# A hybrid decoder layer: the recurrent heads' values and gates from seven block products ahead of the heads, and their elementwise work spread over three engines

## The chip, the core and the metric

The kernel runs on one core of a Trainium2 chip. TensorE (PE) multiplies matrices and turns tiles (a transpose is a matmul with the identity), with its weight loads shown apart (PEld). VectorE (DVE), ScalarE (ACT) and GpSimd (POOL) do elementwise work, SyncE (SP) issues DMAs. PE writes into PSUM, 8 banks of 128 x 512 floats; DVE and ACT read it. The rest lives in SBUF, 128 partitions wide. The metric is the device time of one execution in microseconds. It is compared as a median of several runs; the profile is of one execution.

## What is computed

One decoder layer for 1024 tokens of width 1024, in float32. The part in front of the feed-forward block has two mixers side by side, fed by one projection of the normalised input:

```python
h = rmsnorm(x, mix_pre_norm)
proj = h @ w_in
q_a, k_a, v_a, q_h, f_h, i_h, g_h = split(proj)      # 3 x 512 attention, 4 x 512 recurrence
attn = rmsnorm(dilated_mixture_attention(q_a, k_a, v_a), attn_out_norm)
rec = hgrn2_recurrence(q_h, f_h, i_h, g_h, lb, hgrn_out_norm)
x = x + rmsnorm(concat([attn, rec]) @ w_out, mix_post_norm)
x = x + rmsnorm(square(relu(rmsnorm(x, mlp_pre_norm) @ w_ff1)) @ w_ff2, mlp_post_norm)
```

The recurrence has 4 heads of 128 columns; `f` is the forget gate per key column, `i` the values, `g` the output gate:

```python
f = lb + (1 - lb) * sigmoid(f_h)
S[t] = diag(f[t]) @ S[t-1] + outer(1 - f[t], i[t])
o[t] = S[t].T @ silu(q_h[t])
y = rmsnorm_per_head(o) * silu(g_h)
```

## The kernel before

The order of all instructions is written out by hand; there is no scheduler that moves them. Each engine runs its own list in order and waits on semaphores.

**Three-pass products.** A float32 operand is split into a rounded part `hi` (ACT copies it into the float32r type) and a rest `lo` (a subtraction, on DVE where nothing else is said): `split_into`, L82 to L84. A product is then hi x hi + hi x lo + lo x hi, three matmuls (`three_pass`, L87 to L89). Weights come as a `stream` of 512 KB pieces: `w_load` issues a DMA, `w_split` splits a piece, `w_get(i)` makes sure that piece i, and the next one, are split.

**Opening (0 to 39 us).** The 8 row tiles of x (`xr`, 128 x 1024) are turned by PE as they are (`x_turn`, L257); ACT and DVE take the turned tiles out as `hTh` and `hTl`, scaled by the norm's gain per column. The norm's factor per row, `rstd0`, is only ready later and is multiplied into what is projected: per token block for i and gate, and as a whole row tile `rrow` for q, f and the attention's projections. In the same stage head 0's i and gate columns are made, `pig`, 128 tokens x 256 columns at a time over 8 k: 192 matmuls of 128 x 256.

**Recurrent heads (39 to 307 us).** `hgrn_ig(h)` makes a head's i and gate, `hgrn_qf(h)` its q (with silu, `qt`) and f (`kt`, `tot`, and `prod` = qt x kt). A 1024-token projection of 128 columns, `proj_t`, is 2 halves x 8 k x 3 = 48 matmuls of 128 x 512. `hgrn_core(h)` is the recurrence. In heads 0 to 2 it joins the tokens in three steps by four (c = 1, 4, 16): at each step `quarter_sets` prepares the right-hand sides `qs` (ACT copies, L404 and L408; DVE products with the running gates `tot`, L409 and L411), PE makes 8 score blocks `pl` (L441), DVE copies them under masks into `at` (`copy_predicated`, L473), and DVE scales `qt` (L454, L457), makes the joined gates (L461 to L463) and scales `kt` (L466 to L468). Head 3 goes by two in seven levels (L502 to L513). After the steps come the transposed keys `pk`, state updates `pu` and `st` (L538), the output `po` (L549, L551), its squares `ysq`, and the gated, normalised result (L563), sent to DRAM.

The head's own matmuls wait for DVE between steps. So `fill(ns)` weaves other matmuls between them: it takes pieces from generators in `queue`, each piece one k step with its cost in ns, until the given time is used up. In head h the generators are `hgrn_ig(h+1)` and `hgrn_qf(h+1)`; in head 3 the first attention pair's projections, `attn_proj(0)`. The steps' `sets` of the next step are made before the masked copies of this one.

**After 307 us** follow the attention (to 555), the output projection (to 631), the feed-forward's two products (to 1207.6) and the last norm. The change touches of these only how attention's q, k and v leave PSUM.

Of the kernel before, what the change touches and what calls it, by code (L numbers as in the profile page):

```python
# [17 lines left out]
P = 128  # L18
# [9 lines left out]
LEVELS = (1, 2, 4, 8, 16, 32, 64)  # L28


def f32(ap):
    return ap.bitcast(F32)
# [3 lines left out]
def hymba_layer(ctx, tc, x, w_in, w_out, w_ff1, w_ff2, g_pre, lb_logits, g_mix, g_post,  # L36
# [10 lines left out]
    ps = ctx.enter_context(tc.tile_pool(name="psum", bufs=1, space=PSUM))  # L47
    dp = ctx.enter_context(tc.tile_pool(name="spill", bufs=1, space=DRAM))
# [5 lines left out]
    def bank(tag, name):  # L54
        return ps.tile([P, 512], F32, tag=tag, name=name,
                       bufs={"mm": 2, "s": 2, "t": 2, "pv": 2}[tag])
# [66 lines left out]
    def w_get(i, ahead=1):  # L123
        while done[1] < min(i + 1 + ahead, len(stream)):
            w_split()
        return parts[i]

    def pair_dest(name):
        box = {}

        def dest(j):
            def make():
                if j == 0:
                    box["h"] = slab("V8", f"{name}h", F32R, (P, 2, T))
                    box["l"] = slab("V8", f"{name}l", F32R, (P, 2, T))
                return box["h"][:, j], box["l"][:, j]
            return make
        return dest, box

    def ig_view(box, k):  # L140
        return tuple(box[q].rearrange("p j (k c) -> p j k c", k=NK)[:, :, k] for q in ("h", "l"))

    wig = []
    for h in range(HH):
        dest, box = pair_dest(f"wig{h}")
        wig.append(box)
        for j in range(2):
            stream.append((w_in[4 * h + j], dest(j)))
        for j in range(2):
            stream.append((w_in[4 * h + 2 + j], None))  # L150
    for i in range(4 * HH, 4 * HH + 3 * (AH // 2)):
        stream.append((w_in[i], None))
# [51 lines left out]
    hT = blocks_of("hT")  # L204
# [3 lines left out]
    xrows = [slab("S", f"xr{t}") for t in range(NT)]  # L208

# [3 lines left out]
    nc.sync.dma_start(out=ident, in_=ident_in)  # L213
    x_load(0)
    nc.sync.dma_start(out=gpre, in_=g_pre)
    w_load()
    w_load()
    for t in range(1, NT):
        x_load(t)
    V.memset(ones, 1.0)  # L220
    V.memset(nhalf, -0.5)
    rrow = slab("R", "rrow")
    mraw = slab("T", "mraw", F32, (P, len(LEVELS), 64))
    nc.sync.dma_start(out=lbl, in_=lb_logits)
    nc.sync.dma_start(out=mraw, in_=level_masks)

    mix_dram = dp.tile([T, D], F32, name="mixd")
    x2_dram = [dp.tile([P, D], F32, name=f"x2d{t}") for t in range(NT)]

    def ig_evac(hd, pm, blocks):  # L230
        for u, t in enumerate(blocks):
            S.activation(hd["inat"][:, t], pm[:, u, 0], AF.Copy, scale=rstd0[:, t:t + 1])
            V.tensor_scalar(hd["gate"][:, t], pm[:, u, 1], rstd0[:, t:t + 1], None, op0=ALU.mult)

    def silu_gate(h, gate):
        sg = slab("P", f"sg{h}", F32, (P, NT, P))
        S.activation(sg, gate, AF.Sigmoid)
        V.tensor_tensor(out=gate, in0=gate, in1=sg, op=ALU.mult)

    def new_head(h):  # L240
        return {"inat": slab("T", f"inat{h}", F32, (P, NT, P)), "gate": slab("T", f"gate{h}", F32, (P, NT, P))}

    heads = [None] * HH
    heads[0] = new_head(0)

    PAIRED = ((0, 1), (2, 4), (3, 5), (6, 7))
    pms0 = [bank(tag, f"pig0_{q}").rearrange("p (t j c) -> p t j c", t=2, j=2)
            for q, tag in enumerate(("mm", "mm", "pv", "pv"))]
    place = {t: pms0[q][:, u] for q, pair in enumerate(PAIRED) for u, t in enumerate(pair)}
    turned = [0]  # L250

    def x_turn(t0, n, k):
        hi, lo = part_tok(hT, k, t0, n)
        pt = bank("t" if turned[0] % 2 else "s", f"xt{t0}_{k}")[:, :n * P]
        turned[0] += 1
        for j in range(n):
            TE.transpose(pt[:, j * P:(j + 1) * P], xrows[t0 + j][:, k * P:(k + 1) * P], ident)  # L257
        S.activation(hi, pt, AF.Copy, scale=gpre[:, k:k + 1])
        V.scalar_tensor_tensor(lo, pt, gpre[:, k:k + 1], f32(hi), op0=ALU.mult, op1=ALU.subtract)

    def x_mm(t0, n, k):
        for t in range(t0, t0 + n):
            three_pass(place[t], part_tok(hT, k, t), ig_view(wig[0], k), k == 0, k == NK - 1)

    def squares(t0, n):
        for t in range(t0, t0 + n):
            dump = slab("P", f"sq{t}")
            S.activation(dump, xrows[t], AF.Square, accum_out=ssq0[:, t:t + 1])

    def row_scale(hf):  # L270
        sl = slice(hf * 512, hf * 512 + 512)
        pt = bank("t", f"rb{hf}")
        for j in range(4):
            t = hf * 4 + j
            TE.transpose(pt[:, j * P:(j + 1) * P], rstd0[:, t:t + 1].to_broadcast([P, P]), ident)
        S.activation(rrow[:, sl], pt, AF.Copy)

    def keep_warm(n):

        for _ in range(n):  # L280
# [1615 lines left out]
```

## Time and profile before

| what | us |
| --- | --- |
| median of 3 runs (lowest, highest) | 1261.32 (1260.96, 1261.83) |
| span of the profiled execution | 1258.5 |
| opening ends (head 0's i and gate done) | 39.3 |
| head 0's core begins | 62.5 |
| heads 1, 2, 3 begin | 125.2, 188.7, 252.1 |
| attention begins | 307.1 |
| output projection, ff1, ff2 begin | 555.0, 631.0, 941.0 |

The span runs from the first to the last instruction; about 2.8 us of the median lie around it. The stages are read off PE's list: where the matmuls of one name give way to those of the next. In the profile's rows `L87 PE MATMUL f<-bh,ah 128*128 128x512` means line 87, engine, operation, the tile written and those read, the stationary tile and the moving one; `x392` counts them, and the time of "idle before" belongs to the engine just before such an instruction, with what ended it. `PEclk` and the last columns of a stage row are the granted clock of PE, the busy share of the DMA engines and the GB/s they moved.

### The profile page before, as it was taken

The numbers are of one execution on the slowest core, as the hardware profiler recorded it, in microseconds if no ns is written. First come the engines' busy times: TensorE is split into PE (matmuls) and PEld (weight loads), VectorE is DVE, ScalarE is ACT, GpSimd is POOL, SyncE is SP. The second block draws the span as 40 slices with busy tenths as digits, with TensorE's granted clock in tenths as the row PEclk, the third lists the DMA queues.
The fourth block names the chain that finished last, engine by engine and source line by source line (L and its number), as shares of the span: only waits on it lengthen the run. The fifth ranks groups of instructions, "written<-read, shape, count | busy, mean of one in ns | idle before, by whom it ended". The sixth has DMA issues, their size and how long they took to land. (4 is left out here: it accounts for less than half of the span.)

```text
span 1258.5 us, 17252 instructions
## 1 busy us (share of the span) xinstructions
PE 1235.4 (98%) x6512; PEld 1056.1 (84%) x6512; DVE 884.6 (70%) x1535; ACT 531.9 (42%) x970; POOL 300.6 (24%) x303
## 2 busy tenths in 40 slices
PE   8999999999999999999999999999999999999997
PEld 8898989888888887878878788888878888888886
DVE  5686868675666667668759756666685777698966
ACT  7523232222555556666565322222237434444412
POOL 0000000012222223146250487656621000000012
PEclk9999999999999999999999999999999999999999
DMA  5201111122322224245242545434468454434423
GB/s 210 68 18 51 34 52 34 35 84 64 89 71 81 69 83 132 81 133 184 101 150 81 207 164 184 155 135 172 149 249 324 167 198 134 162 92 132 162 89 118
DMA packets 58578, 153.98 MB, mean 122 GB/s; under 512 B 4992, under 2 KB 12928, under 8 KB 58240
## 3 DMA queue, kind: packets, MB, share of 16 engines
q1 hardware_dynamic: 58496, 152.89, 36.0%
q8 instruction: 51, 0.84, 0.3%
q14 instruction: 31, 0.25, 0.1%
HBM read 106.73 MB, written 39.85 MB: 116 GB/s over the span
## 5 line engine op out<-in xcount | busy, mean ns | idle before, releaser
L87 PE MATMUL f<-bh,ah 128*128 128x512 f32 x392 | 152.5, 389 | 0.0
L88 PE MATMUL f<-bl,ah 128*128 128x512 f32 x392 | 152.5, 389 | 0.0
L89 PE MATMUL f<-bh,al 128*128 128x512 f32 x392 | 152.5, 389 | 0.0
L84 DVE TENSOR_TENSOR al<-ar,ah 128x1024 fp32r<-128x1024 f32 x49 | 60.7, 1238 | 48.1 <-ACT ah L83 19.4
L89 PEld LDWEIGHTS f<-bh,al 128*128 128x128 f32 x392 | 73.6, 188 | 15.4
L87 PEld LDWEIGHTS f<-bh,ah 128*128 128x128 f32 x392 | 73.6, 188 | 15.3
L88 PEld LDWEIGHTS f<-bl,ah 128*128 128x128 f32 x392 | 73.6, 188 | 15.1
L83 ACT ACTIVATE ah<-ar 128x1024 fp32r<-128x1024 f32 x49 | 52.1, 1063 | 50.2 <-PE f L89 25.3
L1814 POOL TENSOR_SCALAR fp<-fss 128x1 f32<-128x1 f32 x8 | 3.7, 462 | 269.4 <-ACT fd L1810 269.4
L734 DVE TENSOR_TENSOR ptl<-pt,pth 128x512 fp32r<-128x512 f32 (+2 forms) x96 | 50.4, 553 | 23.4 <-ACT pth L733 23.3
L733 ACT ACTIVATE pth<-pt 128x512 fp32r<-128x512 f32 (+2 forms) x96 | 43.3, 487 | 40.0 <-PE pt L730 38.5
L706 DVE CUSTOM_DVE_ANT_0 p<-ps,bt 128x512 f32<-128x512 f32 (+2 forms) x84 | 44.4, 554 | 18.3 <-PE ps L704 18.1
L1313 POOL TENSOR_TENSOR e<-x,e 128x512 f32<-128x512 f32 x14 | 20.6, 1475 | 136.0 <-DVE x L1264 136.0
L79 POOL TENSOR_SCALAR ms<-hss 128x8 f32<-128x8 f32 x4 | 0.8, 198 | 209.2 <-DVE hss L554 209.2
L717 ACT ACTIVATE p<-p,nm 128x128 f32<-128x128 f32 (+3 forms) x64 | 49.4, 772 | 2.5 <-DVE nm L710 2.1
L83 ACT ACTIVATE bh<-br 128x1024 fp32r<-128x1024 f32 x28 | 29.8, 1064 | 43.1 <-PE f L89 37.7
L763 POOL TENSOR_TENSOR anat<-anat,rd 128x128 f32<-128x128 f32 x32 | 14.7, 461 | 131.8 <-DVE anat L762 130.9
L730 PE MATMUL pt<-ident,p 128*128 128x128 f32 x288 | 42.7, 275 | 2.7 <-DVE ptl L734 1.6
L747 PE MATMUL pov<-pth,v 128*128 128x256 f32 (+1 forms) x160 | 40.3, 287 | 1.3 <-ACT pth L733 1.3
L1667 DVE TENSOR_TENSOR acc<-f,acc 128x512 f32<-128x512 f32 x52 | 33.8, 686 | 8.2 <-PE f L89 8.2
L730 PEld LDWEIGHTS pt<-ident,p 128*128 128x128 f32 x288 | 33.3, 141 | 7.2 <-DVE ptl L734 3.5
L83 ACT ACTIVATE bh<-tt 128x1024 fp32r<-128x1024 f32 x21 | 22.3, 1061 | 38.2 <-PE f L89 22.9
(1622 smaller groups left out, 3902.3 us busy)
## 6 DMA issues: line engine op xcount, KB each, us to landing
ar<-actd SPq DMA_DIRECT2D x49, 512.0 KB, 3.7
raw<-in_w_in_dram SPq DMA_DIRECT2D x28, 512.0 KB, 3.6
w1r<-in_w_ff_dram SPq DMA_DIRECT2D x14, 1024.0 KB, 6.2
br<-in_w_ff_dram SPq DMA_DIRECT2D x14, 1024.0 KB, 7.9
actd<-e SPq DMA_DIRECT2D x17, 768.0 KB, 4.1
actd<-e SPq DMA_DIRECT2D x11, 1024.0 KB, 4.0
xr<-in_x_dram SPq DMA_DIRECT2D x8, 512.0 KB, 8.6
raw<-in_w_out_dram SPq DMA_DIRECT2D x8, 512.0 KB, 3.6
```

What stands on the lines that cost most here:

```text
L83: S.activation(hi, src, AF.Copy)
L84: eng.tensor_tensor(out=lo, in0=src, in1=f32(hi), op=ALU.subtract)
L87: TE.matmul(dst, lhs[0], rhs[0], start=start, stop=False)
L88: TE.matmul(dst, lhs[0], rhs[1], start=False, stop=False)
L89: TE.matmul(dst, lhs[1], rhs[0], start=False, stop=stop)
L706: V.tensor_tensor_reduce(out=pe[:, k0:k0 + n], in0=pS[:, :n], in1=bts[hd][:, o:o + n], scale=1.0, scalar=-3.0e38, op0=ALU.add, op1=ALU.max ...
L717: S.activation(pe[:, :nk], pe[:, :nk], AF.Exp, bias=nm[:, b:b + 1], accum_out=dn[:, b:b + 1])
L730: TE.transpose(pt[:, j * P:(j + 1) * P], pe[:, jj * P:(jj + 1) * P], ident)
L733: S.activation(hi, src, AF.Copy)
L734: V.tensor_tensor(out=lo, in0=src, in1=f32(hi), op=ALU.subtract)
L747: TE.matmul(po[:, c0:256], vst, pt[j // 4][q][:, j % 4, c0:], start=j == 0 and q == 0, stop=j == nj - 1 and q == 1)
L1667: V.tensor_tensor(out=acc_at(p, i), in0=pm, in1=acc_at(p, i), op=ALU.add)
```

## The change

- **Rows first.** Each row tile is squared (ACT, tile 1 on DVE), its factor is made on POOL, and the row is scaled by DVE before PE turns it. `rrow` and all multiplications with it go.
- **Seven block products.** i and gate of all four heads are one product of 1024 tokens x 1024 by 1024 x 1024 columns. It is cut into 2 x 2 blocks of 512 and made by seven block products instead of eight (Strassen's scheme in Winograd's form): sums and differences of blocks of the rows (`s1` to `s4`) and the weights (`T1` to `T4`), split like every operand, then 7 x 4 token tiles x 4 k x 3 passes. The weight differences T3, T2 and T4 and the row sums are POOL's (`w_diff`, `a_rebuild`, L495, L505), the splits' rests DVE's. The results, i and silu(gate), go to DRAM (`i_dram`, `g_dram`); `head_load` reads a head's columns back as `inat` and `gate`.
- **Less to weave.** `hgrn_ig` is gone. In head h only f of head h+1 and q of head h+2 are left to weave in, and in head 2 two units of the attention's projection. A table, `FILLING`, gives each place its own time.
- **Heads' elementwise work.** The products `prod` and qt x tot, and the three scalings of `kt` per step, go to POOL; f's affine steps to ACT. The gating is made by ACT copies with a scale and a POOL product, and put off into the next head's first step. `ysq` is summed by ACT. The score blocks lie in pairs of banks, so that one masked copy takes 128 x 256. Head 3 goes by four, too.

```diff
+FILLING = (
+    dict(f0=1300.0, f1=700.0, st=(5400.0, 5400.0, 3400.0), f6=1300.0, pk=1400.0, pu=1400.0, po=700.0, end=700.0),
...
+    dict(f0=700.0, f1=0.0, st=(6100.0, 6100.0, 5400.0), f6=1300.0, pk=2000.0, pu=1400.0, po=700.0, end=700.0),
+    def w_diff(dst, in0, in1, eng, which=(0, 1)):
+        for q in which:
+            eng.tensor_tensor(out=wraw[dst][q], in0=wraw[in0][q], in1=wraw[in1][q], op=ALU.subtract)
+    def prod(banks_, toks, a, b, first, last):
+        for i in toks:
+            dst = banks_[i].rearrange("p (h c) -> p h c", h=HH)
+            for k in range(4):
...
+                TE.matmul(dst, lhs[0], rhs[0], start=st, stop=False, skip_group_check=True)
+                TE.matmul(dst, lhs[0], rhs[1], start=False, stop=False, skip_group_check=True)
+                TE.matmul(dst, lhs[1], rhs[0], start=False, stop=sp_, skip_group_check=True)
+                yield
+    def row_stat(t):
...
+            S.activation(dump, xrows[t], AF.Square, accum_out=ssq0[:, t:t + 1])
+        rsqrt_mean(rstd0[:, t:t + 1], ssq0[:, t:t + 1], D, 1)
+    def row_scale(t):
...
+            V.tensor_scalar(xrows[t], xrows[t], rstd0[:, t:t + 1], None, op0=ALU.mult)
+    def a_rebuild(name, kh):
...
+            G.tensor_tensor(out=out_[q], in0=f32(hT["h", kh, 0][:, 2 * q:2 * q + 2]),
+                            in1=f32(hT["l", kh, 0][:, 2 * q:2 * q + 2]), op=ALU.add)
...
+    run_all(p2)
+    w_diff("T2", "B11", "T3", G)
+    a12 = a_rebuild("a12r", 1)
+    send_c11((2, 3))
+    s2 = a_open("s2", "S")
+    run_all(prod(abank, range(2), s3, "T3", True, False))
...
+    w_both("T2", 1)
+    for q in range(2):
+        a_half(s2, s2r, q)
+    run_all(prod(abank, range(2, 4), s3, "T3", True, False))
...
+    for q in range(2):
+        G.tensor_tensor(out=a11[q], in0=a11[q], in1=s2r[q], op=ALU.add)
+    run_all(prod(abank, range(2), s2, "T2", False, False))
...
+        G.tensor_tensor(out=a12[q], in0=a12[q], in1=s2r[q], op=ALU.subtract)
...
+    w_diff("T4", "T2", "B21", G)
...
+            S.activation(tot[:, sl], box[0], AF.Sigmoid)
+            S.activation(kt[:, sl], box[0], AF.Sigmoid, scale=-1.0)
+            S.activation(tot[:, sl], tot[:, sl], AF.Identity, scale=omlb[:, h:h + 1], bias=lb[:, h:h + 1])
+            S.activation(kt[:, sl], kt[:, sl], AF.Copy, scale=omlb[:, h:h + 1])
+            G.tensor_tensor(out=hd["prod"][:, sl], in0=qt[:, sl], in1=kt[:, sl], op=ALU.mult)
+            G.tensor_tensor(out=qt[:, sl], in0=qt[:, sl], in1=tot[:, sl], op=ALU.mult)
...
+            KE[h].tensor_tensor(out=k4[:, :, 2], in0=k4[:, :, 2], in1=spread(cw[:, :, 3]), op=ALU.mult)
+            KE[h].tensor_tensor(out=k4[:, :, 1], in0=k4[:, :, 1], in1=spread(u23), op=ALU.mult)
+            KE[h].tensor_tensor(out=k4[:, :, 0], in0=k4[:, :, 0], in1=spread(u123), op=ALU.mult)
+            while put_off_gate:
+                put_off_gate.pop()()
...
+            fill(scale["st"][step])
...
+        def gated():
...
+                    S.activation(sq[:, g4 * 4 + n], pos[g4][:, n], AF.Copy, scale=rs[:, g4 * 4 + n:g4 * 4 + n + 1])
+                (V if h == HH - 1 else G).tensor_tensor(out=gate[:, g], in0=sq[:, g], in1=gate[:, g], op=ALU.mult)
...
+        queue += [early_attn] if last else [hgrn_f(h + 1)] + ([hgrn_q(h + 2)] if h + 2 < HH else [])
```

`KE` is POOL (`G`) for every head. Three places show how the engines' lists now stand.

POOL in the opening, between the fourth and the sixth block product (a row gives the line, the operation, the tile written and the tiles read, and the size; `a11r` and `a12r` are rebuilt row blocks, `wrT3` holds T3, then T2, then T4, one after the other):

```order
L270 TENSOR_TENSOR wrT3_371<-wrB110_131,wrT3_371 128x1024
L270 TENSOR_TENSOR wrT3_371<-wrB111_133,wrT3_371 128x1024
L367 TENSOR_TENSOR a12r0_502<-hTh10_93,hTl10_94 128x1024
L367 TENSOR_TENSOR a12r1_503<-hTh10_93,hTl10_94 128x1024
L495 TENSOR_TENSOR a11r0_365<-a11r0_365,s2r0_125 128x1024
L495 TENSOR_TENSOR a11r1_366<-a11r1_366,s2r1_126 128x1024
L505 TENSOR_TENSOR a12r0_502<-a12r0_502,s2r0_125 128x1024
L505 TENSOR_TENSOR a12r1_503<-a12r1_503,s2r1_126 128x1024
L270 TENSOR_TENSOR wrT3_371<-wrT3_371,wrB210_137 128x1024
L270 TENSOR_TENSOR wrT3_371<-wrT3_371,wrB211_139 128x1024
```

Before, POOL's list had at this place four small instructions for `rstd0` and nothing else.

DVE at the same place, from the rests of T2 (`wbl`) and of s2 to those of T1 (`wal`) and s1:

```order
L108 TENSOR_TENSOR wbl0_192<-wrT3_371,wbh0_191 128x1024
L108 TENSOR_TENSOR wbl1_194<-wrT3_371,wbh1_193 128x1024
L108 TENSOR_TENSOR s2l0_514<-s2r0_125,s2h0_512 128x512 x2
L108 TENSOR_TENSOR s2l1_515<-s2r1_126,s2h1_513 128x512 x2
L270 TENSOR_TENSOR wrB12_145<-wrB12_145,wrB110_131 128x1024
L270 TENSOR_TENSOR wrB12_145<-wrB12_145,wrB111_133 128x1024
L108 TENSOR_TENSOR wal0_184<-wrB12_145,wah0_183 128x1024
L108 TENSOR_TENSOR wal1_186<-wrB12_145,wah1_185 128x1024
L108 TENSOR_TENSOR s1l_611<-a11r0_365,s1h_610 128x1024
L108 TENSOR_TENSOR s1l_611<-a11r1_366,s1h_610 128x1024
```

These are twelve instructions that all read two tiles in SBUF. Before, DVE took turned tiles out of PSUM here, and two weight pieces.

DVE in head 0, from the joined gates of step 0 to the first masked copies; first before:

```order
L461 TENSOR_TENSOR tot0_848<-tot0_697 128x256
L462 TENSOR_TENSOR tot0_848<-tot0_697,tot0_848 128x256
L463 TENSOR_TENSOR tot0_848<-tot0_697,tot0_848 128x256
L409 TENSOR_TENSOR qs0_10_867<-qt0_626,tot0_848 128x4x8x4
L411 TENSOR_TENSOR qs0_10_867<-qs0_10_867,tot0_848 128x4x64
L409 TENSOR_TENSOR qs0_11_872<-qt0_626,tot0_848 128x4x8x4
L411 TENSOR_TENSOR qs0_11_872<-qs0_11_872,tot0_848 128x4x64
L466 TENSOR_TENSOR kt0_696<-kt0_696,tot0_697 128x256
L467 TENSOR_TENSOR kt0_696<-kt0_696,tot0_848 128x256
L468 TENSOR_TENSOR kt0_696<-kt0_696,tot0_848 128x256
L473 COPY_PREDICATED at0_834<-masks_78,pl0_00_849 128x128
```

and now:

```order
L691 TENSOR_TENSOR tot0_1128<-tot0_943 128x256
L692 TENSOR_TENSOR tot0_1128<-tot0_943,tot0_1128 128x256
L693 TENSOR_TENSOR tot0_1128<-tot0_943,tot0_1128 128x256
L699 TENSOR_TENSOR qt0_880<-qt0_880,tot0_943 128x256
L702 TENSOR_TENSOR qt0_880<-qs0_00_1083,tot0_943 128x128x2
L702 TENSOR_TENSOR qt0_880<-qs0_01_1088,tot0_943 128x128x2
L643 TENSOR_TENSOR qs0_10_1148<-qt0_880,tot0_1128 128x4x8x4
L645 TENSOR_TENSOR qs0_10_1148<-qs0_10_1148,tot0_1128 128x4x64
L643 TENSOR_TENSOR qs0_11_1153<-qt0_880,tot0_1128 128x4x8x4
L645 TENSOR_TENSOR qs0_11_1153<-qs0_11_1153,tot0_1128 128x4x64
L712 COPY_PREDICATED at0_1114<-masks_81,pl0_00_1129 128x256
```

The scalings of `kt` are gone from DVE's list; they are on POOL's, which in head 0 now reads (with `prod1` and `qt1` of the next head between the steps):

```order
L694 TENSOR_TENSOR kt0_942<-kt0_942,tot0_943 128x256
L695 TENSOR_TENSOR kt0_942<-kt0_942,tot0_1128 128x256
L696 TENSOR_TENSOR kt0_942<-kt0_942,tot0_1128 128x256
L622 TENSOR_TENSOR prod1_1095<-qt1_1013,kt1_1093 128x512
L623 TENSOR_TENSOR qt1_1013<-qt1_1013,tot1_1094 128x512
L694 TENSOR_TENSOR kt0_942<-kt0_942,tot0_1128 128x64x4
L695 TENSOR_TENSOR kt0_942<-kt0_942,tot0_1128 128x64x4
L696 TENSOR_TENSOR kt0_942<-kt0_942,tot0_1128 128x64x4
```

The head's `qt` scalings (L699, L702) now stand behind the joined gates instead of ahead of them, and POOL's list, which had nothing but `hrs` in a head, stands beside DVE's.

More of the change, by code (lines that the diff above doesn't have):

```diff
@@ L214, in hymba_layer @@
[L214 to L248, printed above, removed]
@@ L265, in squares @@
[L265 to L278, printed above, removed]
-        for _ in range(n):
-            TE.matmul(pms0[3].rearrange("p t j c -> p (t j c)")[:, :256], warm[:, :P], warm[:, :256],
-                      start=True, stop=True)
@@ new lines, in step, with run_all @@
+    def step(gen, n=1):
+        for _ in range(n):
+            next(gen, None)
+    def run_all(gen):
+        for _ in gen:
+            pass
+    nc.sync.dma_start(out=ident, in_=ident_in)
+    x_load(0)
+    nc.sync.dma_start(out=gpre, in_=g_pre)
+    x_load(1)
+    w_block("B11", 0, 0, ("T", "T"))
+    x_load(2)
+    x_load(3)
+    w_block("B21", 0, 1, ("T", "T"))
+    for t in range(4, NT):
+        x_load(t)
+    w_block("B12", 1, 0, "V8")
+    w_block("B22", 1, 1, ("S", "T"))
+    nc.sync.dma_start(out=lbl, in_=lb_logits)
@@ new lines, in hymba_layer @@
+    p2 = prod(abank, (2, 3), A12, "B21", False, True)
+    step(p1, 8 - BT0)
+    keep_p1((2,))
+    s3 = a_open("s3", "A")
+    for n in range(BT0):
+        step(p1)
+        back_turn(n)
+        if n == 2:
+            a_half(s3, s3r, 0)
+    keep_p1((3,))
+    for n in range(BT0, 4):
+        step(p2)
+        back_turn(n)
+    w_open("T3", 0)
+    a_half(s3, s3r, 1)
+    w_half("T3", 0)
+    w_half("T3", 1)
+    send_c11((0, 1))
+    for n in range(4, 8):
+        step(p2)
+        back_turn(n)
```

606 lines of the change are left out of this document (381 added, 225 removed).

## The prediction

> **What bounds the kernel now.** The page comes first: how much of the span has the matmul engine at work, and which engines have room.
>
> ```profile
> span 1258.5 us, 17252 instructions
> PE 1235.4 (98%) x6512; PEld 1056.1 (84%) x6512; DVE 884.6 (70%) x1535; ACT 531.9 (42%) x970; POOL 300.6 (24%) x303
> POOL 0000000012222223146250487656621000000012
> ```
>
> PE is busy for 98% of the span, so only a shorter list of matmuls can save much. POOL has nothing to do in its first eight slices, and that is where the change puts work. Next come the stages (window, its length, then busy us of PE, PEld, DVE, ACT, POOL; clock, DMA share, GB/s): start and first tokens, opening, head 0's q and f, heads 0 to 3.
>
> ```profile
> 0.00:10.00 10.00, 6.76 (x25) 5.00 (x26) 3.60 (x12) 5.16 (x13) 0.19 (x4) 1.00 0.77 263
> 10.00:39.30 29.30, 29.30 (x249) 29.20 (x250) 18.45 (x47) 24.00 (x58) 1.55 (x2) 1.00 0.34 137
> 39.30:62.50 23.20, 23.08 (x106) 18.61 (x105) 14.13 (x25) 12.68 (x22) 0.90 (x2) 1.00 0.28 91
> 62.50:125.20 62.70, 62.27 (x422) 57.35 (x421) 46.93 (x112) 19.45 (x44) 1.84 (x2) 1.00 0.10 34
> 252.10:307.10 55.00, 54.14 (x333) 47.83 (x332) 35.98 (x58) 12.26 (x18) 8.75 (x6) 1.00 0.28 77
> ...
> PE pl L441 <- DVE at L473: 2.2, 7, 0.3
> PE po L549 <- DVE st L538: 0.9, 1, 0.9
> ```
>
> The last two rows are PE's waits between 39 and 320 us (total, times, longest): 3.1 us in all four heads. DVE is busy 47 us of a head's 63, and some 45 us of projections woven between the head's own matmuls cover its chain. Heads 1 and 2 look like head 0, and everything the change touches ends at 307.1 us.
>
> **The matmuls.** PE's timeline gives the cost of one from start to start.
>
> ```profile
> 72.30 0.28 PE L89 MATMUL pig<-wig1h,hTl 128*128 128x256 f32 x1
> ...
> 75.89 0.28 PE L89 MATMUL pig<-wig1h,hTl 128*128 128x256 f32 x1
> ...
> 261.40 0.39 PE L88 MATMUL pm_aq<-hTl,wh 128*128 128x512 f32 x1
> ...
> 265.05 0.39 PE L89 MATMUL pm_aq<-hTh,wl 128*128 128x512 f32 x1
> ```
>
> Thirty steps lie between the first two: 0.120 us for a 128x256. Sixteen lie between the others: 0.228 for a 128x512. The old i and gate products are 4 x 192 of the first, 768 x 0.120 = 92 us. The new ones are 7 block products x 4 token tiles x 4 k x 3 passes = 336 of the second, 76.6 us. PE saves about 15 us, its one sure gain.
>
> Opening without any wait: in 10.0 to 39.3 us PE has 192 products (23.0 us) and 57 others, nearly all transposes, so one of those costs about 0.11; 64 are 7 us. Products began at about 10 us; now a row is squared, its root taken and the row scaled before it is turned. Three rows price that:
>
> ```profile
> L83 ACT ACTIVATE wh<-raw 128x1024 fp32r<-128x1024 f32 x2 | 2.1, 1051 | 0.0
> L80 POOL TENSOR_TENSOR x2r<-ms,nhalf 128x1 f32<-128x1 f32 x8 | 4.9, 607 | 0.7
> L387 DVE TENSOR_SCALAR tot<-tot,omlb,lb 128x512 f32<-128x512 f32 x2 | 1.1, 547 | 1.4 <-ACT tot L385 1.4
> ```
>
> About 1 us on ACT for a row, 0.8 on POOL with its other small step, twice 0.55 on DVE: 10 + 3 = 13 us. So 13 + 76.6 + 7 = 97 us, and I write 99 for small gaps (before: 39.3).
>
> Heads without any wait: 39.3 to 62.5 us holds two projections and 8 transposes, so a projection is (23.1 - 0.9) / 2 = 11.1 us. Head 0's own work is 62.3 - 23.0 - 2 x 11.1 = 17 us. Afterwards: eight recurrent projections and the three of the first attention pair, 11 x 11.1 = 122, and four heads, 68 (head 3 is now like the others; its 54.1 less three projections is 21): 190 us. So attention would start at 289 instead of 307.1; with the 3 us of waits of before, 292: **15 us saved if nothing new waits**.
>
> **What waits now: DVE and POOL.** The trace shows what happens when both add or multiply data in SBUF. First two stretches (start, duration), then the same kinds of operation alone.
>
> ```profile
> 261.31 0.69 DVE L506 TENSOR_TENSOR kt<-kt,tot 128x512 f32<-128x512 f32 x1 [0.57 <-PE pl L502]
> 261.92 1.78 DVE L508 TENSOR_TENSOR qt<-qt,tot 128x512 f32<-128x512 f32 x1
> 263.63 1.77 DVE L512 TENSOR_TENSOR tot<-tot 128x512 f32<-128x512 f32 x1
> ...
> 261.49 3.37 POOL L618 TENSOR_TENSOR ql<-qf,q 64x512 fp32r<-64x512 f32 x2 [11.66 <-ACT q L617]
> ...
> 772.93 2.20 DVE L84 TENSOR_TENSOR wd7l<-w1r,wd7h 128x1024 fp32r<-128x1024 f32 x1 [2.88 <-ACT wd7h L83]
> 776.79 0.69 DVE L1283 TENSOR_TENSOR x<-f17b,x 128x512 f32<-128x512 f32 x1
> ...
> 773.99 2.28 POOL L1316 TENSOR_TENSOR e<-e,e 128x512 f32<-128x512 f32 x1
> 776.23 1.75 POOL L1200 TENSOR_TENSOR ss<-w1r 128x512 f32<-128x512 f32 x1
> 778.05 1.29 POOL L1201 TENSOR_TENSOR ss<-ss,w1r 128x512 f32<-128x512 f32 x1
> ...
> L84 DVE TENSOR_TENSOR wl<-raw,wh 128x1024 fp32r<-128x1024 f32 x2 | 2.4, 1222 | 0.1
> L763 POOL TENSOR_TENSOR anat<-anat,rd 128x128 f32<-128x128 f32 x32 | 14.7, 461 | 131.8 <-DVE anat L762 130.9 <-POOL ql L618 0.8
> ```
>
> A 128x512 multiply on DVE takes 0.69 us, but 1.78 when POOL began first, and then POOL's second one stretches in its turn: they take turns, each for a whole instruction. A 128x1024 split goes from 1.22 to 2.20, a POOL sum from 1.29 to 2.28. The DVE row at 776.79 reads PSUM (f17b) and keeps its 0.69 beside POOL. So time on POOL is not free: **DVE pays one POOL instruction for each of its own that meets a busy POOL.**
>
> The Trainium skill, page "SBUF — State Buffer", section "🔬 SBUF: two separate sides", speaks against the change here: the pair of ports that the two share is an exclusive lock, held for the whole instruction by whichever started first, and it counts DVE operations with two SBUF inputs among those that take it. The rows agree. By that rule the moves to POOL cost what the next two parts add; were it not to hold, the sum would stay at the 15 us saved.
>
> POOL's prices: 0.46 for 128x128 and 1.29 for 128x512 are shown; between them, 128x256 is about 0.74. A 128x1024 is not shown: twice 1.29 is 2.6, by the slope 2.4; I take 2.4.
>
> *Opening.* POOL gets 18 sums of 128x1024 (rebuilt blocks, differences of weight and row blocks, gates) and a few more splits: 45 to 53 us. DVE's 20-odd splits of 1.22 also have two SBUF inputs. The two collide where PE has least in hand: during s3 x T3, 16 steps of three matmuls, 16 x 0.69 = 11 us. DVE must then split T2 (2) and s2 (4 halves) for the next product, while POOL holds a queue of eight sums that it can start at once. Six DVE instructions x (0.6 to 1.2 own + 2.4 POOL) = 20 us. By the sums so far DVE begins them when PE has some 5 us of that product left, since T3's own splits come just ahead on it, and PE can start the next product on s2's first half, some 3 us early: 20 - 5 - 3 = 12 us of waiting. Smaller ones: T3's halves 1.3, the first rows (a POOL split) 1. **Opening 99 + 14 = 113 us.** Ends: 98, if POOL's sums fall between DVE's, and 117.
>
> *Heads.* The rows of head 0's chain on DVE and ACT:
>
> ```profile
> L473 DVE COPY_PREDICATED at<-masks,pl 128x128 f32<-128x128 uint8 x24 | 8.4, 351 | 0.4
> L411 DVE TENSOR_TENSOR qs<-qs,tot 128x256 f32<-128x256 f32 x6 | 2.6, 426 | 0.6
> L457 DVE TENSOR_TENSOR qt<-qs,tot 128x256 f32<-128x256 f32 x6 | 2.3, 418 | 0.0
> L409 DVE TENSOR_TENSOR qs<-qt,tot 128x128 f32<-128x128 f32 x6 | 1.9, 320 | 0.1
> L454 DVE TENSOR_TENSOR qt<-qt,tot 128x256 f32<-128x256 f32 x3 | 1.5, 497 | 0.0
> L428 DVE TENSOR_TENSOR at<-ident,dg 128x1024 f32<-128x1024 f32 x1 | 1.2, 1225 | 0.0
> L461 DVE TENSOR_TENSOR tot<-tot 128x256 f32<-128x256 f32 x1 | 0.6, 621 | 0.0
> L441 PE MATMUL pl<-qs,kt 128*128 128x192 f32 x48 | 8.8, 330 | 0.4 <-DVE at L473 0.3
> ```
>
> From the sums of pd to the last scaling of kt DVE now has: at 1.2; two splits 2.4; totals 3 x 0.62 and, for the shorter ones, about 1.4; q 3 x (0.50 + 2 x 0.42) = 4.0; qs 2 x 2 x (0.32 + 0.43) = 3.0; six masked copies of 128x256 a step instead of twelve of 128x128. Those are bounded by half of before's time (twelve x 0.35 / 2 = 2.1) and all of it (4.2): I take 4.2 for the first step, whose pieces are single elements, and 2.4 for the others, 9.0. With 0.7 + 0.5 for the last scalings the chain is **24 us**. PE has over the same stretch 3 x 2.5 of pl (8.8 less overlap), fills of 0.7 + 5.4 + 5.4 + 3.4, 1.3 and one more unit: **24 to 25 us**. Before, fills of 7.0 a step covered it; now nothing is left over, and what DVE loses to POOL appears as waits of PE.
>
> It loses per head: nine kt products on POOL (three a step, beside DVE's q products) 9 x 0.74 = 6.6, less one that meets nothing; in heads 1 and 2 the put-off gating, 2 x 1.29; of the eight prod and qt products of a neighbouring f about 1.5. Eight, 10 and 9.5 us for heads 0 to 2; head 3 has longer fills (6.1, 6.1, 5.4) and no gating on POOL: 5.5. Sum 33 us. Ends: 0, if POOL's turns fall under the masked copies, which read PSUM, and 4 x 11 = 44. **Heads 190 + 33 = 223 us**, less the 3 us of old waits, which these replace.
>
> The other edits go together: head_load reads 512 KB back per head, far ahead of its use; f's scalings move to ACT, which has 40 us to spare per head; attention's q and v copies go from DVE to ACT. I cost them at nothing, and 1 us each way if a cover is gone.
>
> **Sum.** 113 + 223 = 336 us against 307.1: 29 us more. The profiled execution, 1258.5, becomes 1287.5, and the median lies 2.8 above the span: **1290 us**.
>
> **Rivals.**
> - *The cover holds.* POOL's turns fall under PSUM reads and ACT copies, so the saved matmuls show: 98 to 102 plus 190 to 200, against 307.1, is 5 to 19 us less: 1242 to 1256 us. For it speaks that DVE, busy 47 us of a head, loses work to POOL and ACT; against it, that the rows show every meeting costing a whole instruction. It decides if the next pl starts within 8 us of the one before in step 0.
> - *The lock bites in one place only*, opening (14 us) or heads (33 less what longer fills absorb, about 18): 1258 to 1278 us.
> - *The clock.* A long idle of PE is followed by half clock once:
>
> ```profile
> 503.26 0.85 PE L848 MATMUL pmt<-ident,erows 128*128 128x128 f32 x4 [2.93 <-POOL erows L808]
> 503.60:507.00 3.40, 3.40 (x11) 2.72 (x10) 0.70 (x2) 0.89 (x2) 2.88 (x3) 0.50 1.05 285
> ```
>
> Each wait of 3 us could so add 1.7 us (half of 3.4). With one to six such waits the forecast goes to 1292 to 1300. The Trainium skill, page "TensorE: Matmul & The Clock Gate", section "What's actually happening", halves the rate after an idle window of about 3.4 us, so waits shorter than that need not trigger it, and by it alone the forecast stays 1290; the row shows the halving after 2.93.
> - *The change does not do what it says*: the seven products are 336 matmuls by the program's own order, so only lost overlap could undo the saving, which is the forecast.
>
> **How the numbers follow.** The lock in both places, with or without the clock: 0.58, 1274 to 1304. One place: 0.17, 1258 to 1278. Cover holds: 0.25, 1242 to 1258. The last tenth below 1250 and a few per cent above 1304 are left out: 1250 to 1304. A difference within 0.2% (1258.8 to 1263.8) is about what a measurement of this kernel cannot tell from none. It lies inside the second case: 0.07. So 0.25 faster, 0.07 same, 0.68 slower.
>
> **What would show it.** Right: PE waits of some 10 us in the opening that end with s2's split, DVE splits of 2 us and more, and PE waits for masked copies and for qs in each head; attention starting near 336 us. Wrong: DVE's splits at 1.2 us throughout, waits of PE below 5 us before attention, which then starts near 292; or a gap that a DMA ends.

## The result, and the profile after

The changed kernel takes 1296.8 us (median of 4, 1294.75 to 1301.86) against 1261.3 (1260.96 to 1261.83): a ratio of 1.0287, 95% interval 1.0266 to 1.0308, 35.5 us more. 1290 with a range of 1250 to 1304 had been forecast. The profiled execution is the longest of the four, 1301.86, so its stages show some 5 us more than the median run has. One execution of the ninth run below took 1777.9 us at a mean granted clock of 0.65, against 0.99 in its other three, and is left out of its median.

The head of the page of the changed kernel, as it was read before:

```profile
span 1300.1 us, 16370 instructions
PE 1238.2 (95%) x6036; PEld 1036.9 (80%) x6036; DVE 896.1 (69%) x1387; ACT 566.4 (44%) x1047; POOL 427.0 (33%) x395
POOL 3843234334322121424523087665651000000012
PEclk8979999988999999999999999999999999999999
```

PE has 476 instructions fewer and yet is busy longer (1238.2 against 1235.4 us), and its clock has dips in the first ten slices, where before there were none:

```profile
PEclk9999999999999999999999999999999999999999
```

Stages of the changed kernel (opening; q and f ahead of head 0's core; the four cores; from attention on):

```profile
0.00:119.50 119.50, 102.71 (x427) 81.00 (x428) 83.18 (x83) 55.23 (x82) 60.56 (x39) 0.90 0.30 108
119.50:154.40 34.90, 34.56 (x152) 28.28 (x152) 11.34 (x17) 13.14 (x22) 11.79 (x6) 1.00 0.38 121
154.40:350.30 195.90, 166.94 (x916) 145.49 (x914) 137.02 (x255) 68.29 (x189) 71.23 (x67) 0.94 0.20 57
350.30:1300.10 949.80, 933.94 (x4546) 782.16 (x4545) 664.61 (x1034) 429.74 (x756) 283.46 (x283) 1.00 0.42 141
```

The kernel before, cut where head 0's own matmuls begin (`pd`, at 66.2 us, the mark used for the changed kernel too; the 62.5 of the earlier table is where the first woven ones begin) and at attention. Its first row holds opening, q and f:

```profile
0.00:66.20 66.20, 62.84 (x406) 56.48 (x407) 38.76 (x87) 43.65 (x96) 2.64 (x8) 1.00 0.37 132
66.20:307.10 240.90, 237.71 (x1564) 216.04 (x1563) 175.30 (x396) 67.80 (x145) 14.79 (x12) 1.00 0.16 47
307.10:1258.50 951.40, 934.84 (x4547) 783.61 (x4545) 670.51 (x1053) 420.46 (x729) 283.17 (x283) 1.00 0.42 141
```

From attention on, the two agree within 2 us (949.8 and 951.4). All of the loss is ahead of it: attention begins at 350.3 instead of 307.1. Up to there PE is idle for 46.1 us (350.3 less its busy time of 304.2) where it was for 6.5. Its longest waits in the changed kernel:

```profile
PE pl L678 <- DVE at L712: 18.7, 4, 6.2
PE piga L284 <- DVE s2l L108: 6.5, 4, 3.1
PE xt L312 <- DVE xr L304: 5.0, 3, 3.2
PE pk L739 <- DVE tot L728: 3.4, 4, 1.7
```

They are the two that the prediction named (s2's split in the opening, the masked copies in each head) and a third, the scaled rows at the start, for which it had 1 us. The fourth row, the wait for the keys, comes back below.

**Turns in the opening.** DVE's and POOL's lists while PE waits for s2 (start, duration):

```profile
57.74 6.22 DVE L108 TENSOR_TENSOR wbl<-wrT,wbh 128x1024 fp32r<-128x1024 f32 x2
63.89 11.12 DVE L108 TENSOR_TENSOR s2l<-s2r,s2h 128x512 fp32r<-128x512 f32 x4
...
57.15 5.74 POOL L367 TENSOR_TENSOR a12r<-hTh,hTl 128x1024 f32<-128x1024 f32 x2
62.83 6.10 POOL L495 TENSOR_TENSOR a11r<-a11r,s2r 128x1024 f32<-128x1024 f32 x2
68.89 5.58 POOL L505 TENSOR_TENSOR a12r<-a12r,s2r 128x1024 f32<-128x1024 f32 x2
```

Six splits take 17.3 us. Each of s2's four, 0.68 us alone, lasts 2.8: one sum of POOL each.

**Turns in head 1.** The same two lists behind the first step's score blocks, and the wait that ends it on PE:

```profile
206.48 1.54 DVE L699 TENSOR_TENSOR qt<-qt,tot 128x256 f32<-128x256 f32 x1
207.94 2.10 DVE L702 TENSOR_TENSOR qt<-qs,tot 128x256 f32<-128x256 f32 x2
209.97 1.38 DVE L643 TENSOR_TENSOR qs<-qt,tot 128x128 f32<-128x128 f32 x1
...
206.30 1.25 POOL L694 TENSOR_TENSOR kt<-kt,tot 128x256 f32<-128x256 f32 x1 [4.04 <-PE pl L678]
209.72 2.75 POOL L784 TENSOR_TENSOR gate<-ysq,gate 128x512 f32<-128x512 f32 x2
...
216.89 4.52 PE L678 MATMUL pl<-qs,kt 128*128 128x192 f32 x16 [5.20 <-DVE at L712]
```

The next score blocks can only start when the masked copies have emptied a bank, the copies stand behind the scalings of qt, and those take turns with POOL's scalings of kt and the gating.

**The clock.** Behind such a wait PE is slow for a while; here in the opening (a window, then PE's rows in it):

```profile
66.00:80.00 14.00, 9.88 (x21) 6.42 (x22) 14.00 (x6) 1.06 (x1) 14.00 (x6) 0.53 0.00 0
...
66.77 0.80 PE L284 MATMUL piga<-wbh,s2l 128*128 128x512 f32 x1 [3.11 <-DVE s2l L108]
67.36 0.63 PE L282 MATMUL piga<-wbh,s2h 128*128 128x512 f32 x1
67.78 0.63 PE L283 MATMUL piga<-wbl,s2h 128*128 128x512 f32 x1
```

From start to start a matmul takes 0.42 us instead of 0.228. Counted in windows of 1.5 us by their granted clock, PE runs at half speed for about 48 us ahead of attention.

### The profile page after: what moved, and what is told of

The parts are those of the page before. It is cut to its first block, busy times and chain, and to the rows that moved or that the text cites. A ratio compares the mean times of both kernels' runs of the same rounds, so it can differ in the third digit from the quotient of the medians.

```text
span 1300.1 us, 16370 instructions
## 1 busy us (share of the span) xinstructions
PE 1238.2 (95%) x6036; PEld 1036.9 (80%) x6036; DVE 896.1 (69%) x1387; ACT 566.4 (44%) x1047; POOL 427.0 (33%) x395
## 5 line engine op out<-in xcount | busy, mean ns | idle before, releaser
L678 PE MATMUL pl<-qs,kt 128*128 128x192 f32 x192 | 41.7, 380 | 20.0 <-DVE at L712 18.7
L678 PEld LDWEIGHTS pl<-qs,kt 128*128 128x128 f32 x192 | 38.8, 227 | 22.5 <-issue 21.1
L108 DVE TENSOR_TENSOR wl<-raw,wh 128x1024 fp32r<-128x1024 f32 x22 | 28.2, 1282 | 35.4 <-ACT wh L107 35.3
L107 ACT ACTIVATE bh<-br 128x1024 fp32r<-128x1024 f32 x28 | 29.8, 1064 | 42.8 <-PE f L113 37.5
```

Source lines behind the costliest of these rows:

```text
L107: S.activation(hi, src, AF.Copy)
L108: eng.tensor_tensor(out=lo, in0=src, in1=f32(hi), op=ALU.subtract)
L678: TE.matmul(pl[:, n % 4, :192], kt[:, n * P:(n + 1) * P], sets[u][:, n % 4], start=True, stop=True)
```

## The experiments

Stages below are read off each run's PE list, like those above: where the opening ends (the start of its last matmul), and the us from there to attention ("heads", with the q and f ahead of them). Each row's stages are those of one profiled execution, and these vary: three kernels with the same heads (the change, the third and the fifth run) show 230.8, 225.5 and 225.0, so 5 us between two rows of "heads" say little.

| kernel | median us | ratio to before (95%) | opening ends | heads |
| --- | --- | --- | --- | --- |
| before | 1261.3 | | 39.2 | 267.9 |
| the change | 1296.8 | 1.0287 (1.0266 to 1.0308) | 119.5 | 230.8 |
| e1_left_out | 1274.5 | 1.0101 (1.0081 to 1.0120) | 115.8 | 204.8 |
| e2_copies_first | 1287.6 | 1.0212 (1.0192 to 1.0232) | 115.0 | 218.5 |
| e3_hold_pool | 1293.7 | 1.0259 (1.0239 to 1.0279) | 115.9 | 225.5 |
| e4_warm | 1298.2 | 1.0288 (1.0264 to 1.0311) | 119.3 | 225.0 |
| e5_opening | 1291.1 | 1.0233 (1.0213 to 1.0253) | 112.5 | 225.0 |
| e6_heads_two | 1296.8 | 1.0272 (1.0244 to 1.0299) | 117.5 | 228.0 |
| e7_no_pool | 1291.4 | 1.0230 (1.0210 to 1.0250) | 117.3 | 219.6 |
| e8_both | 1288.7 | 1.0219 (1.0197 to 1.0241) | 109.5 | 225.3 |
| e9_combined | 1279.1 | 1.0137 (1.0109 to 1.0166) | 104.9 | 220.9 |
| e10_combined_late | 1292.8 | 1.0248 (1.0216 to 1.0280) | 107.4 | 232.3 |
| e11_no_turns | 1259.4 | 0.9983 (0.9967 to 0.9999) | 101.0 | 202.5 |
| e12_late_only | 1278.7 | 1.0131 (1.0113 to 1.0148) | 105.3 | 220.7 |

**First: POOL's part in the steps left out.**

```diff
-            KE[h].tensor_tensor(out=k4[:, :, 2], ...)
-            KE[h].tensor_tensor(out=k4[:, :, 1], ...)
-            KE[h].tensor_tensor(out=k4[:, :, 0], ...)
...
-                (V if h == HH - 1 else G).tensor_tensor(out=gate[:, g], in0=sq[:, g], in1=gate[:, g], op=ALU.mult)
+                if h == HH - 1:
+                    V.tensor_tensor(out=gate[:, g], in0=sq[:, g], in1=gate[:, g], op=ALU.mult)
```

> The changed kernel without POOL's part in the steps: the three scalings of kt per step and the gating product of heads 0 to 2 are left out, so the recurrence's values are other ones; DVE's, ACT's and PE's lists stay as they are. Turn-taking theory: in step 0 DVE's qt scalings fall from 1.54 and 2 x 1.05 us to 0.50 and 2 x 0.42, PE's waits for the masked copies in the heads from 18.7 us to under 4, and the half-clock stretches behind them go; the time falls by 20 to 32 us from 1296.8, to 1265 to 1277. Rival (too little is woven in, whatever POOL does): the waits stay above 12 us and the time above 1285.

1274.5 us, inside the range. DVE's list is the same, and its rows at the same place in head 1 are:

```profile
198.21 0.61 DVE L696 TENSOR_TENSOR qt<-qt,tot 128x256 f32<-128x256 f32 x1
198.74 0.75 DVE L699 TENSOR_TENSOR qt<-qs,tot 128x256 f32<-128x256 f32 x2
199.41 0.28 DVE L643 TENSOR_TENSOR qs<-qt,tot 128x128 f32<-128x128 f32 x1
```

Four operations take 1.6 us; with POOL beside them they took 5.0 (1.54, 2.10, 1.38). PE's waits for the masked copies fall from 18.7 to 1.7 us:

```profile
PE pl L678 <- DVE at L709: 1.7, 3, 0.6
```

So the waits come with the work that POOL was given, and without it the woven matmuls are enough. But what is left out here is work that somebody has to do; the seventh run gives it back to DVE.

**Second: masked copies ahead of the scalings of qt** (the loop over `banks4` moved up, nothing else).

> The changed kernel with the masked copies of a step put ahead of the scalings of qt and the next sets, so that DVE reads PSUM while POOL scales kt and gates. Turn-taking theory: the copies run beside POOL at their own pace (4.4 us in step 0 against POOL's 2.3 to 5), qt's scalings then meet an idle POOL, and PE's waits in the heads fall from 29 us to 8 to 15: 1270 to 1283 us. Rival (the length of DVE's list decides, not what stands beside it): the next score blocks wait for the sets in place of the copies, and the time stays within 1290 to 1300.

1287.6 us: 9 less, short of the range expected. Head 1's first step, DVE and POOL:

```profile
201.61 1.52 DVE L703 COPY_PREDICATED at<-masks,pl 128x256 f32<-128x256 uint8 x2
...
201.41 1.27 POOL L694 TENSOR_TENSOR kt<-kt,tot 128x256 f32<-128x256 f32 x1 [4.02 <-PE pl L678]
204.27 2.56 POOL L784 TENSOR_TENSOR gate<-ysq,gate 128x512 f32<-128x512 f32 x2
...
PE pl L678 <- DVE qs L645: 7.4, 5, 2.1
PE pl L720 <- DVE qt L710: 6.9, 2, 3.5
```

The copies, which read PSUM, keep their 0.75 us each beside POOL, and POOL's gating its 1.28. That is the mechanism. But the waits only change their name, as the rival had it: the score blocks now wait for the next sets (7.4 us), and the last ones for qt (6.9). In head 1's last step POOL's qt x tot of the next head, which it makes ahead of kt's scalings, meets DVE's joined gates (2.4 us for three short operations), and DVE waits 2.0 us for a weight's copy on ACT. How much each of the two costs is not shown.

**Third: POOL's sums held back until s2 is split.**

```diff
+    G.tensor_scalar(col("hold", 1), f32(s2[3][1][:, 511:512]), 1.0, 0.0, op0=ALU.mult, op1=ALU.add)
...
-    a12 = a_rebuild("a12r", 1)
+    a_rebuild("a12r", 1, a12)
```

> The changed kernel with POOL's eight sums behind T2 in the opening held back until DVE has split s2 (POOL first reads one element of s2's last rest). Turn-taking theory: DVE's six splits take 6 us instead of 17, PE's waits for s2 fall from 6.5 us to under 1.5, and the half clock from 66 to 80 us goes: 9 to 13 us less, 1284 to 1288. Rival (the sums are themselves urgent, so that s1 or s4 come late by as much): 1293 to 1300.

1293.7 us. The six splits of T2 and s2:

```profile
56.41 2.34 DVE L108 TENSOR_TENSOR wbl<-wrT,wbh 128x1024 fp32r<-128x1024 f32 x2
58.68 2.49 DVE L108 TENSOR_TENSOR s2l<-s2r,s2h 128x512 fp32r<-128x512 f32 x4
```

They take 4.8 us instead of 17.3, and PE does not wait for s2 at all. Of the 9 to 13 us only about 3 arrive: the held sums then take turns with T1's and s1's splits (6.8 and 6.7 us for two each), and PE waits 4.9 us for a bank that DVE empties (`ww`) right behind s1's splits, and 2.3 later for one behind s4's. Mechanism as expected, gain mostly passed on; the rival's time.

**Fourth: idle transposes on PE where it waits.**

```diff
             fill(scale["st"][step])
+            if step == 0:
+                dm = bank("pv", f"dm{h}")
+                for _ in range(16 if h == 0 else 40):
+                    TE.transpose(dm[:, :P], ident, ident)
```

> The changed kernel with idle transposes (16 in head 0, 40 in the others, 0.11 us each) on PE behind the first step's woven matmuls, where it waits 2 to 6 us for the masked copies; nothing waits for them. Clock theory: the half-clock stretches behind these four waits go, and each gives back about half of its 3.4 to 6.8 us: 5 to 9 us less, 1288 to 1292. Rival (PE would wait for DVE anyway, the slow clock falls into waiting): 1295 to 1298, with the clock restored.

1298.2 us (1295.2 to 1299.5): no gain, on the rival's side. The half clock behind the four waits is gone (in heads some 7 us of it are left, of 24 in the change and 20 in the third and fifth run), but the heads' 225.0 us are those of the third and fifth run, whose heads are the change's. So in the heads a slow PE mostly spends time in which it would wait for DVE. In heads 0 to 2 the transposes end before the copies that PE waits for; in head 3 they run some 2 us past them (to 313.7, the copies to 311.8), so a gain of that size could be hidden.

**Fifth: another order of the opening's sums.**

```diff
-            w_lo("B21", n // 2, G)
+            w_lo("B21", n // 2, V)
...
-        G.tensor_tensor(out=a11[q], in0=a11[q], in1=s2r[q], op=ALU.add)
+        V.tensor_tensor(out=a11[q], in0=a11[q], in1=s2r[q], op=ALU.add)
...
+    G.tensor_scalar(col("hold", 1), f32(s1[3][1][:, 511:512]), 1.0, 0.0, op0=ALU.mult, op1=ALU.add)
+    w_diff("T4", "T2", "B21", G)
+    a_rebuild("a12r", 1, a12)
...
-    w_diff("T4", "T2", "B21", G)
```

> The changed kernel with the opening's sums ordered anew: a11 + s2 on DVE; POOL held back until DVE has split s1 and only then making T4, the rebuilt a12 and its difference; B21's two rests on DVE. Turn-taking theory: no DVE split between 50 and 72 us meets a busy POOL, PE's waits for s2 and s1 (7 us here, 5 us when POOL was held until s2 only) go, and the first wait for a scaled row falls from 3.2 to about 1 us: the opening ends at 104 to 109 us instead of 116 to 120, the time is 1281 to 1287. Rival (the shared time of DVE and POOL is too long wherever it lies): T4 or a12 come late by 5 us or more, 1290 to 1297.

1291.1 us, opening at 112.5: PE runs from 28 to 94 us with one wait of 1.3, and then waits 4.6 for a bank that DVE empties behind s4's two rests, which take 6.7 us beside POOL's first product of the gates. Better than the third run by 3 us, but above the range and at the rival's time: the turns had moved to the one place that the edit had not looked at.

**Sixth: the second run, and prod and qt x tot on DVE.**

```diff
-            G.tensor_tensor(out=hd["prod"][:, sl], in0=qt[:, sl], in1=kt[:, sl], op=ALU.mult)
-            G.tensor_tensor(out=qt[:, sl], in0=qt[:, sl], in1=tot[:, sl], op=ALU.mult)
+            V.tensor_tensor(out=hd["prod"][:, sl], in0=qt[:, sl], in1=kt[:, sl], op=ALU.mult)
+            V.tensor_tensor(out=qt[:, sl], in0=qt[:, sl], in1=tot[:, sl], op=ALU.mult)
```

> Masked copies first (the second run), and in addition the next head's products prod and qt x tot on DVE, where they were on POOL ahead of kt's scalings. Turn-taking theory: DVE has 2.8 us more per head, but kt's scalings no longer queue behind them and no qt scaling meets them: PE's waits for qt before the last score blocks (6.9 us) fall under 2 and the time is 1280 to 1285. Rival (DVE's length decides): 1287 to 1293.

1296.8 us, a miss: 9 us above the second run. PE's waits for sets and qt grow from 7.4 and 6.9 to 10.1 and 9.2 us. Three heads get four products of 0.69 us each, 8.4 us more for DVE, while its scalings of qt and its sets lose 5 us less to POOL (37.8 us busy instead of 42.8). PE's idle time in the heads grows by 3.7 us, and its busy time, at unchanged work, by 5.9: half clock lasts 24 us there instead of 10. DVE's length counts, as the rival had it, but the time lies above the rival's range too, and most of the difference is the clock. (The profiled execution is the slowest of the three, 1298.9.)

**Seventh: all of the heads' POOL work back on DVE** (`KE` to DVE, the two products above, and the gating).

> The changed kernel with everything that it gave to POOL in the heads back on DVE (kt's scalings, prod, qt x tot, the gating product), in the order of the change: 9 x 0.49 + 4 x 0.69 + 2 x 0.69 = 8.6 us more on DVE per head. Turn-taking theory: DVE loses as much to turns as it gains by the move, so the time is 1290 to 1299, about that of the change. Rival (POOL takes the work off DVE, and the waits have another cause): about 6 us more per head, 1310 to 1325.

1291.4 us (1290.0 to 1291.75), below every run of the change. POOL took 8.6 us per head off DVE, and the turns that this brought cost more than it saved. Yet with no product or scaling of the heads on POOL, PE still waits for the masked copies:

```profile
PE pl L678 <- DVE at L712: 10.0, 6, 3.0
```

That is more than half of the change's 18.7 us. Where this work is DVE's own, its list is too long for the matmuls that are left to weave in.

**Eighth: the fifth and the sixth together.**

> The new order of the opening (this call's first kernel) and the two edits of the heads (its second) together. If both act where they are thought to, their gains add: 1296.8 less 10 to 15 and less 12 to 16, 1266 to 1275. If the heads absorb what the opening gains, or the other way round, it stays above 1278.

1288.7 us, a miss, on the rival's side. The opening ends at 109.5, the heads stay at 225.3: the gain is the opening's alone, as the sixth run then leads one to expect.

**Ninth: copies first, the opening's new order, and the gates' product there on DVE.**

```diff
         S.activation(sg, x0[q], AF.Sigmoid)
-        G.tensor_tensor(out=sg, in0=x0[q], in1=sg, op=ALU.mult)
+        V.tensor_tensor(out=sg, in0=x0[q], in1=sg, op=ALU.mult)
```

> Masked copies first (the second run) with the new order of the opening (the fifth), and the gates' first product in the opening on DVE, since it met the split of s4 (4.6 us of waiting there). If the gains add: 1296.8 less 9.2, 5.7 and 4 to 6, 1274 to 1279, with an opening that ends at 106 to 109 us. Rival (one wait takes another's place): 1282 or more.

1279.1 us, 17.7 below the change, at the upper end of the range that was expected. The opening ends at 104.9, and PE waits 2.5 us for the bank behind s4 instead of 4.6.

**Tenth and twelfth: prod and qt x tot behind kt's scalings on POOL**, in the tenth with the diagonal of `at` on ACT as well.

```diff
+            def gates(sl=sl):
+                G.tensor_tensor(out=hd["prod"][:, sl], in0=qt[:, sl], in1=kt[:, sl], op=ALU.mult)
+                G.tensor_tensor(out=qt[:, sl], in0=qt[:, sl], in1=tot[:, sl], op=ALU.mult)
+            put_off_f.append(gates)
...
-        V.tensor_tensor(out=at, in0=ident.unsqueeze(1).to_broadcast([P, NT, P]),
-                        in1=dg.unsqueeze(2).to_broadcast([P, NT, P]), op=ALU.mult)
+        for c in range(NT):
+            S.activation(at[:, c], ident, AF.Copy, scale=dg[:, c:c + 1])
```

> The kernel before it in this call, and in the heads two things more: POOL makes the next head's prod and qt x tot behind kt's scalings, beside the masked copies, instead of ahead of them; and the diagonal of at is made by ACT (8 copies with a scale) instead of DVE. Turn-taking theory: kt's scalings of steps 1 and 2 then start with the copies, no qt scaling meets them, and DVE's chain is 1.2 us shorter: 4 to 8 us less than that kernel, 1267 to 1274. Rival (DVE's own length decides and POOL's place is all one): within 2 us of it.

> The ninth run's kernel (copies first, new opening) with only the second of the tenth run's two edits: POOL makes the next head's prod and qt x tot behind kt's scalings; the diagonal of at is back on DVE. In the tenth run ACT's eight copies for it stood ahead of a weight split for which DVE then waited 3.5 us. If that was what cost 12 us there, and the later products help as thought: 1274 to 1279, 1 to 6 us below the ninth. Rival (the later products themselves are to blame): 1285 or more.

The tenth took 1292.8 us, a miss. ACT's and DVE's lists in its head 1 say why:

```profile
193.91 2.45 ACT L680 ACTIVATE at<-ident,dg 128x128 f32<-128x128 f32 x8 [0.83 <-DVE dg L677]
196.27 1.04 ACT L107 ACTIVATE wh<-raw 128x1024 fp32r<-128x1024 f32 x1
...
197.34 1.23 DVE L108 TENSOR_TENSOR wl<-raw,wh 128x1024 fp32r<-128x1024 f32 x1 [3.46 <-ACT wh L107]
```

A weight's copy on ACT stood behind the eight copies, DVE waited 3.5 us for it, and behind that stood the head's chain: PE's waits for the sets are 17.5 us instead of the ninth run's 8.1. Without the eight copies (twelfth) 1278.7 us were measured, inside the range; its interval overlaps the ninth's, so the later products are not shown to help.

**Eleventh: POOL's work left out in both places** (the first run's, and in the opening the ten sums behind T2, with T2 and s2 split in place of T4 and of a12 - s2; B21's rests on DVE).

> The changed kernel with work of POOL left out in both places, so that the values are other ones: in the heads the scalings of kt and the gating product (as in the first run), in the opening the ten sums behind T2 (the rebuilt a12, a11 + s2, a12 - s2, T4, the gates' first product); B21's rests on DVE. Everything of PE, ACT and DVE stays. Turn-taking theory: the opening ends at 102 to 108 us, the heads take 170, and the time is 1252 to 1264, about that of before or less: what the change saves on PE shows once nobody takes turns. Rival (other limits lie just beneath): 1268 or more.

1259.4 us (median of nine, 1254.9 to 1265.8), inside the range: a ratio of 0.9983 (0.9967 to 0.9999). The profiled execution is the fastest of the nine:

```profile
0.00:101.00 101.00, 92.65 (x427) 75.60 (x428) 69.00 (x92) 55.17 (x84) 27.41 (x27) 1.00 0.37 131
101.00:135.20 34.20, 34.20 (x152) 28.34 (x151) 8.06 (x10) 12.68 (x19) 11.78 (x6) 1.00 0.36 116
135.20:303.50 168.30, 157.71 (x916) 135.99 (x915) 118.54 (x255) 68.25 (x189) 33.56 (x25) 1.00 0.22 67
```

PE's list is that of the change, its clock is full throughout, and attention begins at 303.5, 3.6 us ahead of the kernel before. The other eight executions have mean granted clocks of 0.991 to 0.997, where the profiled one has 0.998, and are 2 to 11 us longer.

## Why the prediction was right, step by step

- **PE's saving, 15 us: right.** The eleventh run has PE's list at full clock: 92.7 + 34.2 + 157.7 = 284.6 us busy ahead of attention, against 62.8 + 237.7 = 300.5 before, 16 us less.
- **The opening without waits, 99 us: right** (101.0 there, with 8.4 us of idle).
- **The heads without waits, 190 us: too low.** PE's busy time there is 191.9, but 10.6 us of idle come on top (303.5 - 101.0 = 202.5), where the prediction counted on at most the old 3. PE now waits for pk's keys and for small steps that the older heads' matmuls covered. This is also why the case in which the cover holds, 1242 to 1256, was too cheerful: even with this work of POOL left out the time falls by about 2 us.
- **Turn-taking: right, in both places.** The third run shows it in the opening (17.3 to 4.8 us for the same six splits), the first in the heads (5.0 to 1.6 us for the same four operations; POOL's work itself is left out there). The second run speaks for turns and against slow memory as such: copies from PSUM run beside the same POOL instructions unchanged.
- **What the turns cost: the sum right, by luck.** 47 us of new waits had been added, 14 in the opening and 33 in the heads, to an attention that would start at 289 without them. By the eleventh run that start is 303.5, and the change's 350.3 is 46.8 later, 18.5 of it in the opening and 28.3 in the heads. But only 27.2 of these are idle time of PE (46.1 less 18.9); the other 19.6 are a slower clock. The waits were put some 20 us too high, the clock stood at nothing in the sum, and the two errors cancel. In the four cores 29.0 us of idle were found (195.9 less 166.9), and 10.6 of them stay in the eleventh run (168.3 less 157.7). In the opening the 12 us for s2 became 6.5 of idle with half clock between. The 47 compare the slowest execution of the change with the fastest of the eleventh run; the medians lie 37.4 apart.
- **The clock: the term that was mis-sized.** It stood as a rival at up to 10 us, one to six stretches of half clock, and not in the sum. PE's busy time ahead of attention is 304.2 us against 284.6 for the same list at full clock: 19.6 us. The 48 us of half clock are some fourteen stretches of 3.4. So the profiled 43.2 are 39.5 of idle (46.1 less 6.5 before) + 19.6 of clock - 16.0 saved = 43.1. The fourth run warns against reading this as 19.6 us to be had: with the clock restored behind the heads' waits the time did not fall.
- **Cover: right, and without turns too.** "Nothing is left over" holds for work that takes no turns as well: with all of the heads' POOL work on DVE the time is still 1291.4, and 10.0 of the 18.7 us of waits for the masked copies are there (seventh run).
- **From span to median: 1 us too much.** The prediction put the median 2.8 us above the span, by spans and times of different executions. In one and the same execution the difference is 1.8 us (1301.86 and 1300.1).
- **The rival "the cover holds"** is refuted by the waits; "the lock bites in one place only" by the first and third run.

No version with the reference's values beat the kernel before. The best, the twelfth run, stays 1.3% above it.

What stays open: how the eleventh run's gain over the ninth (20 us) divides between turns and the mere length of the work that is left out, since leaving it out removes both. The run-to-run spread of the change (7 us against 1 before) may come from the clock: the slowest of its four executions has the lowest mean clock, 0.980 against 0.982 to 0.985. That is argued and was not tried.

## What to carry to other kernels

Matmuls that one saves are only worth what they were not hiding: before taking work off a full PE, sum the chain of the other engines that it covered, and see what is left over; what then waits can cost clock as well as time. An engine that looks idle may still share a resource: moving products of two SBUF tiles from DVE to POOL cost DVE, here, one POOL instruction for every one that met, so give POOL what can run beside DVE's work on PSUM, and look where the turns go next when one place is cleared.

## What the runs showed of the hardware beyond this

**One tile read is enough for turns.** The scaling of a row tile, one SBUF tile and a column of factors, takes 0.75 us alone (0.75 at 33.51 us in the changed kernel) and met POOL's splits:

```profile
21.55 1.82 DVE L304 TENSOR_SCALAR xr<-xr,rstd 128x1024 f32<-128x1024 f32 x1
24.09 2.82 DVE L304 TENSOR_SCALAR xr<-xr,rstd 128x1024 f32<-128x1024 f32 x1 [0.33 <-POOL rstd L104]
...
24.03 2.34 POOL L258 TENSOR_TENSOR wbl<-wrB,wbh 128x1024 fp32r<-128x1024 f32 x1
```

PE's 3.2 us wait at the start ends with the second of these. With the two splits on DVE (fifth run) the scalings there take 0.75 again and the wait is 2.15. So the turn adds 1.0 us, which is what the prediction had for it; the rest of the wait is there without POOL's splits.

**The clock halves after shorter waits than the one seen before.** In head 0 (stage rows):

```profile
163.00:165.80 2.80, 2.80 (x13) 2.01 (x11) 2.59 (x7) 2.24 (x7) 0.87 (x1) 1.00 0.00 0
165.80:168.60 2.80, 0.70 (x5) 0.70 (x5) 2.70 (x5) 1.29 (x2) 1.36 (x2) 1.00 0.01 3
168.80:172.20 3.40, 3.02 (x12) 2.57 (x11) 3.15 (x10) 0.97 (x4) 0.98 (x1) 0.55 0.00 0
```

PE was idle for 2.10 us from 165.8, and in the 3.4 us from 168.8 its mean granted clock was 0.55 (0.50 from 169.5 to 172.5). The prediction's row had 2.93 us of idle. The Trainium skill, page "TensorE: Matmul & The Clock Gate", section "What's actually happening", names an idle window of about 3.4 us; by that, 2.10 would not have been enough. Here the measurement decides.
